# Hybrid RWKV-7, attention and gated-delta trunk on one core: merged recurrence tasks, given out in batches after a set wait, and a builder's clock that charges for changes of tile kind

## The chip, the core and the metric

One core of a Trainium2 chip. The metric is the device time of one execution in microseconds (us). The kernel before took 4177.51 us (median of 3 runs, 4175.42 to 4184.36).

## The reference, cut to what matters

Two layers. In each, one projection `x @ w_in` (1,024 to 4,240 columns) feeds three groups of heads. A layer norm follows the output projection. A prompt of 2,048 tokens and 8 running streams of 16 tokens (the "sample" part, 128 tokens) share the weights.

```
proj = x @ w_in
o_a = rwkv_mix(...)     # RWKV-7: state s <- s*w - (s.kk)(kk*a) + v k ; o = s.r, group norm, bonus
o_b = fox_prompt(...)   # softmax(q.k/8 + c_q - c_k), causal, 8 heads; sample: 1,024 cached rows each
o_c = gdn_mix(...)      # conv(4), silu, l2norm, delta rule in chunks of 64, RMS norm
h = concatenate([o_a, o_b, o_c]) @ w_out
x_new = layer_norm(ALPHA * x + h)
```

## The kernel before, in words

Each layer runs in three stages on TensorE. **Projection with recurrence:** `proj` walks over thirds of the tokens (640, 768, 768) and, for each block of 128 columns of `w_in`, makes 8 x 3 products of 128x128 by 384 (or 320) columns into the PSUM tile `pm`. The operands are split into a high and a low float32r part (`xh`, `xl`, `wh`, `wl`), hence three products. `vgroup` does the same by token block for the value columns (PSUM tile `pv`) and, during it, transposes the input of the next third (`pt`). **Attention:** `fox_prompt` makes `mx` (scores for the row maximum), `st` (scores again, shifted) and `fo` (weights by values). **Output:** `out_proj` makes `op` and the layer norm.

The recurrences of RWKV and gated delta (RG) and then the sample attention (`fox_sample`) are filled in between. They are written as generators, called tasks, one set per block of 256 tokens (`rg_sub`): `rwkv_a`, `gdn_a` prepare, `rwkv_b`, `rwkv_b2`, `gdn_b`, `gdn_b2` build small products, `inverse` and `inverse2` solve a triangular system, `both_chain` steps the state through 64-token chunks, and `rwkv_post`, `gdn_post` norm and gate the result. A task yields the time at which what it waits for is expected, and `step` gives out the next piece of the first task whose time has come.

What sets the order is the builder's own clock, `Model.t`. `PE.add` moves it on by a cost for each product; `Model.op` places every other engine's work against it and gives each instruction a priority from it. TensorE's instructions stay in the order in which the builder emits them during the first two stages; SyncE's DMA issues are ordered by the same clock. `drive` loops over the main work (projection or attention) and, when the clock passes `next_rg`, gives out one piece of a task, then lets the main work have as much of the clock as the piece took (`mix` is 1).

Tasks take PSUM from a ring `gr` of 2 banks for each of their tile names (all of one tag), and SBUF from rings by tag (`RG_TAGS`): `O` and `Ogc` shared one buffer, `Y` had another. Line 221 of the profile is `PE.matmul`, line 224 `PE.transpose`, line 243 every operation of the other engines; groups are therefore told by tiles.

The products of the tasks have several shapes. Of the TensorE rows, `64*64` means 64 rows of weights by 64 columns, `128*128` the whole array. Float32 products appear as two records each, transposes as one.

Of the kernel before, what the change touches and what calls it, by code (L numbers as in the profile page):

```python
# [78 lines left out]
for _tag, _bufs, _names in (  # L79
    ("t7", 1, "pr pc"),  # L80
    ("t7b", 1, "xs"),
    ("ur", 4, "sw a cs Dt kt"),
    ("uw", 1, "th sq n2"),
    ("ug", 2, "sg sqk gm Dm er"),
    ("ui", 1, "Wi T11"),
    ("uo", 1, "O Ogc"),
    ("uc", 1, "Oc so"),
    ("uz", 1, "z"),
    ("u9", 1, "Y"),
    ("m", 1, "strow lst lsto"),  # L90
    ("m2", 2, "lstc"),
    ("q4", 2, "BK DM N am rm km qm SSraw"),
):
    for _n in _names.split():
        RG_TAGS[_n] = (_tag, _bufs)
# [103 lines left out]
class PE:  # L199
    def __init__(self, tc, model):  # L200
        self.tc, self.eng, self.m = tc, tc.nc.tensor, model
        self.keep = False

    def add(self, fn, out, a, b, cyc, first):
        m = self.m
        m.t = max(m.t, m.ready(a, b))
        if first:
            m.t = max(m.t, m.last(out.tensor.name) + m.LAT if out.tensor.name not in m.done else 0.0)
        m.t += cyc / 2400.0
        for x in (a, b):  # L210
            m.used[x.tensor.name] = max(m.used.get(x.tensor.name, 0.0), m.t)
        m.done[out.tensor.name] = m.t + 0.05
        self.tc.cur_priority = int((m.t + 30.0) * 100)
        ins = fn()
        if self.keep:
            self.tc.keep_in_program_order(ins)
# [79 lines left out]
class Trunk:  # L296
# [236 lines left out]
    def proj(self, l, ti, groups, nxt=None):  # L533
# [35 lines left out]
        def vgroup(gi):  # L569
# [32 lines left out]
            if nxt is not None:  # L602
                for j in range(nt - 1, nn):
                    for k in range(2):
                        self.transpose_tile(l, nxt, j, k)
                        yield
# [168 lines left out]
    def rg_sub(self, l, t0, W):  # L775
# [24 lines left out]
        n["Er"] = self.task(self.rwkv_post(x), n["Dr"], n["Dg"], gate)  # L800
        n["Eg"] = self.task(self.gdn_post(x), n["Er"])
# [160 lines left out]
    def rwkv_b2(self, x):  # L962
# [5 lines left out]
        for p in range(2):  # L968
            ps = self.ps("gr", "bkp", 2)
            for c in range(nch):  # L970
                self.pe.transpose(ps[:, c * 128:c * 128 + 128], BK[:, p, c].rearrange("p s t -> p (s t)"), self.ident)
            nc.scalar.copy(BKt[:, p].rearrange("p c h t -> p (c h t)"), ps[:, :nch * 128])
        yield self.w(vv)
        X = self.rt("X", [128, 2, nch, 2, 64])
        ps = self.ps("gr", "vps", 2)
        for p in range(2):
            for w in range(nch // 2):
                q = p * (nch // 2) + w
                self.pe.transpose(ps[:, q * 128:q * 128 + 128], vv[:, p, w * 128:w * 128 + 128], self.ident)
        pv = ps[:, :nch * 128].rearrange("p (q w h t) -> p q w h t", q=2, h=2, t=64)  # L980
# [6 lines left out]
        yield self.w(X, Gk)  # L987
# [6 lines left out]
        Y = self.rt("Y", [128, 2, nch, 64])  # L994
        nc.scalar.copy(Y, yp)
        yield
        if not smp:
            lp = self.ps("gr", "l21", 2)[:, :npc * 32].rearrange("p (q c t) -> p q c t", q=2, t=32)
            for p in range(2):
                for c in range(nch):  # L1000
                    for h in range(2):
                        s = slice(h * 64, h * 64 + 64)
                        self.pe.matmul(lp[h * 64 + 32:h * 64 + 64, p, c], AR[s, p, c, 1, 32:64], BK[s, p, c, h, 0:32], start=True, stop=True)
            L21 = self.l21(x)
            for h in range(2):
                s = slice(h * 64 + 32, h * 64 + 64)
                nc.scalar.copy(L21[s, 0:npc], lp[s].rearrange("p q c t -> p (q c) t"))
        self.m.drop(BK)
        nc.gpsimd.tensor_tensor(kt, kt, r, op=ALU.mult)
        yield self.w(kt)  # L1010
        bp = self.ps("gr", "bonus", 2)[:, :2 * W].rearrange("p (q t) -> p q t", q=2)
        for p in range(2):
            self.pe.matmul(bp[:, p], v["rkm"][:, p], kt[:, p], start=True, stop=True)
        self.m.drop(kt)
# [5 lines left out]
    def gdn_a(self, x):  # L1020
# [61 lines left out]
        yield self.w(smt, sqk)  # L1082
        sp = self.ps("gr", "sps", 2)
        n4 = sp[:, 0:npc].rearrange("p (w q h) -> p w q h", q=2, h=2)
        for w in range(nch // 2):
            for p in range(2):
                self.pe.matmul(n4[:, w, p], sqk[:, p, w * 128:w * 128 + 128], self.k["bdones"][:, 0:128:64], start=True, stop=True)
        self.m.drop(sqk)
        kn, n2, be, ax, ab, g, b = (self.rt(nm, [128, nch, 2], 2) for nm in ("kn", "kn2", "be", "ax", "ab", "gg", "bb"))
        kv = kn.rearrange("p (w e) q -> p w e q", e=2)  # L1090
        for h in range(2):
            for e in range(2):
                nc.vector.tensor_scalar(kv[h * 64:h * 64 + 64, :, e], n4[e * 64:e * 64 + 64, :, :, h], L2_EPS, None, op0=ALU.add)
        nc.vector.tensor_tensor(ax, smt[:, :, 2:4], v["dt_bias"].unsqueeze(1).to_broadcast([128, nch, 2]), op=ALU.add)
        self.sigmoid(be, smt[:, :, 0:2])
        yield
        nc.vector.reciprocal(n2, kn)
        nc.scalar.activation(kn, kn, AF.Ln)
        nc.scalar.activation(kn, kn, AF.Exp, scale=0.5)
        nc.vector.tensor_tensor(b, be, n2, op=ALU.mult)  # L1100
# [5 lines left out]
        yield self.w(g)  # L1106
        gf = g.rearrange("p c q -> p (c q)")
        cp = self.ps("gr", "cps", 2)
        self.pe.matmul(cp[:, 0:npc], x["bdtri"], gf, start=True, stop=True)
        if not smp:  # L1110
            self.pe.matmul(cp[:, 64:64 + npc], self.k["bdtri32"], gf, start=True, stop=True)
        neg = self.rt("neg", [128, nch, 2], 2)
# [7 lines left out]
    def gdn_b(self, x):  # L1120
# [44 lines left out]
        L21 = None if smp else self.l21(x)  # L1165
        for c0 in range(0, nch, 2):
            ps = self.ps("gr", "eqp", 2)
            for c in (c0, c0 + 1):
# [6 lines left out]
            pk = ps.rearrange("p (j e t) -> p j e t", e=2, t=64)  # L1175
# [13 lines left out]
    def gdn_b2(self, x):  # L1189
# [9 lines left out]
        for src, dst in ((vv, Vt), (k, Kt)):  # L1199
            yield self.w(src)  # L1200
            ps = self.ps("gr", "vkp", 2)
            for p in range(2):
                for w in range(nch // 2):
                    j = w * 2 + p
                    self.pe.transpose(ps[:, j * 128:j * 128 + 128], src[:, p, w * 128:w * 128 + 128], self.ident)
            pv = ps[:, :nch * 128].rearrange("p (w q h t) -> p w q h t", q=2, h=2, t=64)
# [308 lines left out]
    def rwkv_post(self, x):  # L1515
        nc, v, W = self.nc, self.rv, x["W"]
        O, Oc = x["O"].rearrange("p q t -> p (q t)"), self.rt("Oc", [128, 2 * W])
        f = lambda t: t.rearrange("p (q t) -> p q t", q=2)
        yield self.w(O)
        mp = self.ps("gr", "mp", 2)[:, :2 * W]  # L1520
        self.pe.matmul(mp, self.k["bdones"], O, start=True, stop=True)
        nc.vector.scalar_tensor_tensor(out=Oc, in0=mp, scalar=-1.0 / 64.0, in1=O, op0=ALU.mult, op1=ALU.add)
        nc.scalar.activation(O, Oc, AF.Square)
        yield self.w(O)
# [3 lines left out]
        nc.scalar.activation(O, O, AF.Exp, scale=-0.5)  # L1528
        nc.vector.tensor_tensor(Oc, Oc, O, op=ALU.mult)
# [3 lines left out]
        self.gate(x, 0, f(Oc), "za")  # L1533
        nc.gpsimd.dma_start(self.OD[x["l"]][0:256, x["t0"]:x["t0"] + W].rearrange("(q p) t -> p q t", p=128), f(Oc))

    def gdn_post(self, x):
        nc, v, W = self.nc, self.rv, x["W"]
        O, Oc = x["Og"].rearrange("p q t -> p (q t)"), self.rt("Ogc", [128, 2 * W])
        f = lambda t: t.rearrange("p (q t) -> p q t", q=2)
        nc.scalar.activation(Oc, O, AF.Square)  # L1540
        nc.gpsimd.tensor_tensor(Oc, Oc, x["q2"].rearrange("p q t -> p (q t)"), op=ALU.add)
        yield self.w(Oc)
        mp = self.ps("gr", "gmp", 2)[:, :2 * W]
        self.pe.matmul(mp, self.k["bdones"], Oc, start=True, stop=True)
        nc.scalar.activation(Oc, mp, AF.Ln, bias=self.eps["gdn"], scale=1.0 / 64.0)
        nc.scalar.activation(Oc, Oc, AF.Exp, scale=-0.5)
        nc.vector.tensor_tensor(O, O, Oc, op=ALU.mult)
        nc.vector.tensor_scalar(O, O, v["gng"], None, op0=ALU.mult)
        self.gate(x, 768, f(O), "zc")
        nc.gpsimd.dma_start(self.OD[x["l"]][768:1024, x["t0"]:x["t0"] + W].rearrange("(q p) t -> p q t", p=128), f(O))  # L1550
# [519 lines left out]
```

## Time and profile before

| | |
|---|---|
| median of 3 runs | 4177.51 us |
| the profiled execution, its own time | 4169.68 us |
| its span in the profile | 4167.9 us |
| mean granted TensorE clock | 0.954 |
| TensorE busy | 3815.8 us (92%) |
| VectorE, ScalarE, GpSimd busy | 2710.4, 1637.5, 1243.3 us |

The profiled execution stands 7.8 us (0.19%) under the median. The stages of layer 0, by the first and last `pm`, `mx`, `st` and `op` in the trace: projection alone to about 200 us, projection with recurrence to 1351, attention with the rest of the tasks to 1922, output to 2121. Layer 1 follows with the same stages at 2250, 3404 and 3970 us. A busy TensorE row counts modelled ends, so what a product costs is read from start to start.

### The profile page before, as it was taken

How to read it: one execution, taken by the hardware profiler on the slowest of the kernel's cores; microseconds unless marked ns; L12 is line 12 of the kernel's file. 1: busy time of each engine (PE TensorE's matmuls, PEld its weight loads, DVE VectorE, ACT ScalarE, POOL GpSimd, SP SyncE). 2: the span in 40 equal slices, each digit the busy share in tenths (PEclk: the TensorE clock that was granted, in tenths of full speed). 3: DMA queues.
4: the chain of work that ended last, by engine and by line, in shares of the span. 5: the costliest groups of instructions: out<-in, count | busy, mean ns of one | idle time of the engine just before them, and what ended most of it. 6: DMA issues, size and time to landing. Idle time of an engine off the chain costs nothing.

```text
span 4167.9 us, 78031 instructions
## 1 busy us (share of the span) xinstructions
PE 3815.8 (92%) x30554; PEld 3058.0 (73%) x30554; DVE 2710.4 (65%) x6029; ACT 1637.5 (39%) x3351; POOL 1243.3 (30%) x1073
## 2 busy tenths in 40 slices
PE   5889998999988899989998898989999989999998
PEld 5878887888878455546888788978888864554477
DVE  5386567766775776774533857487578747777645
ACT  2253434344353344443123434244444514444411
POOL 3412232222121444444222112312121215444532
PEclk9899999999999899999999999989999989999999
DMA  7743545344544676463455445444445455764333
GB/s 241 222 150 118 151 147 172 117 136 145 161 152 149 155 210 181 119 154 100 150 156 174 150 122 158 154 141 141 135 142 162 155 156 173 197 190 123 88 114 121
DMA packets 601755, 633.81 MB, mean 152 GB/s; under 512 B 153625, under 2 KB 457483, under 8 KB 601387
## 3 DMA queue, kind: packets, MB, share of 16 engines
q1 hardware_dynamic: 598634, 619.90, 49.7%
q0 software_dynamic: 2752, 8.92, 0.6%
q8 instruction: 241, 3.95, 0.4%
q14 instruction: 128, 1.04, 0.1%
HBM read 437.59 MB, written 191.10 MB: 151 GB/s over the span
## 4 chain that ended last, share of the span: by engine, by line
PE 53%; DVE 21%; issue 11%; POOL 5%; DMA 5%; ACT 4%; SPq 1%; POOLq 0%; DVEq 0%; ACTq 0%
PE pm L221 22%; PE st L221 5%; PE fo L221 5%; PE op L221 4%; DVE Wi L243 3%; DVE itmp L243 3%; PE mx L221 3%; PE pv L221 2%; PE cr L221 2%; PE ktp L224 1%; DVE TT L243 1%; PE co L221 1%; PE cg L221 1%; DVE y L243 1%; DVE m L243 1%
## 5 line engine op out<-in xcount | busy, mean ns | idle before, releaser
L221 PE MATMUL pm<-xh,wh 128*128 128x384 f32 (+1 forms) x2784 | 1001.1, 360 | 34.0 <-ACT wh L243 29.1
L221 PE MATMUL pm<-xh,wl 128*128 128x384 f32 (+1 forms) x2784 | 928.7, 334 | 33.1 <-DMA wl<-wd 17.7
L221 PE MATMUL pm<-xl,wh 128*128 128x384 f32 (+1 forms) x2784 | 927.6, 333 | 0.0
L221 PEld LDWEIGHTS pm<-xh,wh 128*128 128x128 f32 x2784 | 537.5, 193 | 78.3 <-ACT wh L243 31.0
L221 PEld LDWEIGHTS pm<-xh,wl 128*128 128x128 f32 x2784 | 536.0, 193 | 38.7 <-DMA wl<-wd 20.2
L221 PEld LDWEIGHTS pm<-xl,wh 128*128 128x128 f32 x2784 | 538.0, 193 | 12.5 <-issue 12.1
L243 POOL TENSOR_TENSOR acc<-acc,pt 128x512 f32<-128x512 f32 (+2 forms) x336 | 382.0, 1152 | 339.9 <-ACT pt L243 307.1
L243 ACT ACTIVATE pt<-st 128x512 f32<-128x512 f32 (+3 forms) x640 | 331.2, 532 | 341.8 <-PE st L221 315.2
L243 DVE TENSOR_REDUCE m<-mx 128x1 f32<-128x512 f32 (+3 forms) x640 | 370.1, 603 | 131.1 <-PE mx L221 128.0
L243 ACT CAST wh<-wr 128x1024 fp32r<-128x1024 f32 (+1 forms) x198 | 207.9, 1051 | 287.4 <-PE pm L221 185.0
L221 PE MATMUL fo<-pt,V 128*64 128x512 f32 (+3 forms) x1280 | 313.3, 570 | 2.4 <-ACT pt L243 1.9
L243 ACT COPY st<-pm 128x384 f32<-128x384 f32 (+1 forms) x348 | 159.0, 458 | 385.6 <-PE pm L221 290.8
L221 PE MATMUL mx<-KA,QA 66*128 66x512 f32 (+3 forms) x640 | 265.1, 435 | 26.2 <-DMA QA<-qs 17.1
L221 PE MATMUL st<-QB,KB 128*128 128x512 f32 (+3 forms) x640 | 277.8, 434 | 8.0 <-DVE m L243 2.9
L221 PE MATMUL st<-QA,KA 104*128 104x512 f32 (+3 forms) x640 | 243.4, 380 | 1.1 <-DVE QA L243 1.1
L243 POOL TENSOR_SCALAR SD<-Sr,dl 128x64 f32<-128x64 f32 x128 | 68.3, 547 | 583.5 <-DVE Sr L243 547.7
L243 POOL TENSOR_TENSOR wl<-wr,wh 128x1024 fp32r<-128x1024 f32 x58 | 141.2, 2435 | 257.6 <-ACT wh L243 222.7
L221 PEld LDWEIGHTS mx<-KA,QA 66*128 66x128 f32 x640 | 126.9, 203 | 123.5 <-issue 78.8
L221 PE MATMUL op<-woh,oh 128*128 128x512 f32 x544 | 211.9, 389 | 0.0
L221 PE MATMUL op<-woh,ol 128*128 128x512 f32 x544 | 211.8, 389 | 0.0
L221 PE MATMUL op<-wol,oh 128*128 128x512 f32 x544 | 211.7, 389 | 0.0
L221 PEld LDWEIGHTS st<-QB,KB 128*128 128x128 f32 x640 | 128.6, 201 | 106.9 <-issue 65.4
(378 smaller groups left out, 7651.6 us busy)
## 6 DMA issues: line engine op xcount, KB each, us to landing
wr<-in_w_in SPq DMA_DIRECT2D x198, 512.0 KB
wl<-wd SPq DMA_DIRECT2D x116, 512.0 KB
kc<-in_cache_fox_k SPq DMA_DIRECT2D x32, 1024.0 KB
vc<-in_cache_fox_v SPq DMA_DIRECT2D x32, 1024.0 KB
wd<-wl SPq DMA_DIRECT2D x58, 512.0 KB
xin<-xd SPq DMA_DIRECT2D x78, 256.0 KB
y<-xd SPq DMA_DIRECT2D x34, 512.0 KB
ol<-od SPq DMA_DIRECT2D x34, 512.0 KB
```

Source lines behind the costliest of these rows:

```text
L221: self.add(lambda: self.eng.matmul(out, a, b, start=start, stop=stop), out, a, b, cyc, start)
L224: self.add(lambda: self.eng.transpose(out, a, ident), out, a, ident, 2 * numel(out), True)
L243: r = f(*a, **b)
```

## The change

Every engine has the same instructions as before (23,152 products on TensorE); their order and some waits differ.

- **Clock.** `PE.add` charges 280 cycles, in the builder's clock alone, where the kind changes: float32r or not, more than 64 rows or not, more than 64 columns or not.
- **Batches.** `drive` asks `due`: it starts a batch when the earliest ready task has been late for 1.5 us of that clock, or is late and no other task comes due within the next 1.5 us. It then gives out pieces until the batch has used 2 us.
- **Merged pieces.** `rwkv_post` and `gdn_post` are one task `post` (it waits for `gdn_b2` too). In `rwkv_b2` the products `l21` move ahead of `yps`, and `bonus` follows `yps` at once. In `gdn_a` the products for the norms and for the cumulated decay come together. `gdn_b` makes both halves of `eqp` before it reads either; `gdn_b2` makes both transposes together. `vgroup` makes the two halves of the next third's transposes in one place (k = 4) instead of two (k = 1 and 5).
- **Buffers.** `Ogc` moves from `O`'s buffer to `Y`'s.

TensorE, the projection during the second block of the prompt. `cr` and `cg` are products of the state chain (`both_chain`), `eqp` of `gdn_b`, `pm` is the main work. Before, a step of the chain is a visit by itself, and each half of `eqp` (`x8`) another, six `pm` ahead of these rows' end and six behind it:

```order
L221 MATMUL pm<-xh,wh 128x384
L221 MATMUL pm<-xl,wh 128x384
L221 MATMUL pm<-xh,wl 128x384
L221 MATMUL cr<-X,BKt 64x64 x4
L221 MATMUL cg<-Xg,Kt 64x64 x4
```

Now:

```order
L224 MATMUL pm<-xh,wh 128x384
L224 MATMUL pm<-xl,wh 128x384
L224 MATMUL pm<-xh,wl 128x384
L224 MATMUL cr<-R,TT 64x64 x4
L224 MATMUL cg<-Rg,TT 64x64 x4
L224 MATMUL eqp<-y 64x128 x16
```

Three visits became one: a step of the chain and both halves of `eqp`.

TensorE, the projection of the value columns, first block of the prompt; `sps` and `cps` are products of `gdn_a`, `yps` and `bonus` of `rwkv_b2`, `pt` the transposes of the next third. Before, `cps` is a visit by itself, and so are `sps` and `yps` ahead of it and `bonus` behind it:

```order
L224 MATMUL pt<-cst,xin 128x128 x4
L221 MATMUL pv<-wh,xh 128x256
L221 MATMUL pv<-wl,xh 128x256
L221 MATMUL pv<-wh,xl 128x256
L221 MATMUL cps<-gg,cst 128x8 x2
```

Now:

```order
L227 MATMUL pt<-cst,xin 128x128 x8
L224 MATMUL pv<-wh,xh 128x256
L224 MATMUL pv<-wl,xh 128x256
L224 MATMUL pv<-wh,xl 128x256
L224 MATMUL sps<-cst,sqk 128x2 x4
L224 MATMUL sps<-gg,cst 128x8 x2
L224 MATMUL yps<-X,Gk 64x64 x16
L224 MATMUL bonus<-kt,rkm 128x256 x2
```

Four visits became one, and `pt` stands eight at a time.

TensorE, the last block of a layer: `mp` and `gmp` are products of the post task, `sfp` of the state's output, `mx` the attention's first maxima. Before:

```order
L221 LDWEIGHTS idb
L221 MATMUL mx<-ngb,idb 128x128
L224 MATMUL sfp<-cst,Sr 64x128 x2
L221 MATMUL mx<-KA,QA_14837 128x512
L221 MATMUL mp<-O,cst 128x512
L221 MATMUL mx<-KA,QA_14837 128x128
```

Now:

```order
L224 MATMUL pm<-xh,wh 128x320
L224 MATMUL pm<-xl,wh 128x320
L224 MATMUL pm<-xh,wl 128x320
L224 MATMUL mp<-O,cst 128x512
L224 MATMUL gmp<-Ogc,cst 128x512
```

The recurrence of a layer now ends inside the projection.

The diff, cut to its core:

```diff
     def add(self, fn, out, a, b, cyc, first):
         m = self.m
+        kind = (a.dtype == F32R, a.shape[0] > 64, out.shape[0] > 64)
+        if kind != self.kind:
+            cyc, self.kind = cyc + 280.0, kind
         m.t = max(m.t, m.ready(a, b))
...
     def drive(self, fill):
         for until in fill:
             if until:
                 self.idle(until)
-            while self.m.t >= self.next_rg:
-                t = self.m.t
-                if not self.step():
-                    break
+            t = self.m.t
+            if t >= self.next_rg and self.due(t):
+                while self.m.t - t < 2.0 and self.step():
+                    pass
                 self.next_rg = self.m.t + self.mix * (self.m.t - t)
+
+    def due(self, t):
+        wakes = [self.wake(q) for q in self.tasks if q.ready()]
+        late = t - min(wakes, default=t + 1.0)
+        return late >= 0.0 and (late >= 1.5 or not any(t < w <= t + 1.5 for w in wakes))
...
-                    if nxt is not None and k in (1, 5):
-                        if j:
-                            self.transpose_tile(l, nxt, j - 1, k // 5)
-                        if j < nn:
-                            self.xin[l, nxt, j, k // 5] = self.load_x(l, nxt, j, k // 5)
+                    if nxt is not None and k == 4:
+                        for half in range(2):
+                            if j:
+                                self.transpose_tile(l, nxt, j - 1, half)
+                            if j < nn:
+                                self.xin[l, nxt, j, half] = self.load_x(l, nxt, j, half)
...
-        n["Er"] = self.task(self.rwkv_post(x), n["Dr"], n["Dg"], gate)
-        n["Eg"] = self.task(self.gdn_post(x), n["Er"])
+        n["Er"] = n["Eg"] = self.task(self.post(x), n["Dr"], n["Dg"], n["Bg2"], gate)
...
-        yield self.w(X, Gk)
+        if not smp:
+            L21 = self.l21(x)
+            for h in range(2):
+                s = slice(h * 64 + 32, h * 64 + 64)
+                nc.scalar.copy(L21[s, 0:npc], lp[s].rearrange("p q c t -> p (q c) t"))
+        self.m.drop(BK)
+        yield self.w(X, Gk, kt)
...
-        yield self.w(smt, sqk)
-        sp = self.ps("gr", "sps", 2)
...
+        yield self.w(g, sqk)
+        cp = self.ps("gr", "sps", 2)
...
+        eqs = []
         for c0 in range(0, nch, 2):
             ps = self.ps("gr", "eqp", 2)
+            eqs.append(ps)
...
+        yield self.w(O, Ogc)
+        mp, gp = self.ps("gr", "mp", 2)[:, :2 * W], self.ps("gr", "gmp", 2)[:, :2 * W]
         self.pe.matmul(mp, self.k["bdones"], O, start=True, stop=True)
+        self.pe.matmul(gp, self.k["bdones"], Ogc, start=True, stop=True)
```

## Rows read from the trace of the kernel before

**Rows 1.** The page's first part: the span, and TensorE's busy time.

```profile
span 4167.9 us, 78031 instructions
PE 3815.8 (92%) x30554; PEld 3058.0 (73%) x30554; DVE 2710.4 (65%) x6029; ACT 1637.5 (39%) x3351; POOL 1243.3 (30%) x1073
```

**Rows 2.** Busy time by stretch: us, PE, PEld, DVE, ACT, POOL, granted clock, DMA share, GB/s.

```profile
200.00:1351.00 1151.00, 1059.83 (x10390) 961.57 (x10391) 782.23 (x2047) 489.94 (x1050) 243.52 (x249) 0.95 0.48 146
1351.00:1457.00 106.00, 87.36 (x427) 46.54 (x426) 77.12 (x145) 35.29 (x66) 50.83 (x48) 0.82 0.60 154
1457.00:1770.00 313.00, 302.84 (x2173) 167.60 (x2173) 228.11 (x432) 150.27 (x286) 135.71 (x118) 0.99 0.61 171
1770.00:1922.00 152.00, 137.13 (x586) 68.67 (x584) 105.75 (x162) 72.99 (x134) 87.16 (x72) 0.93 0.43 110
```

**Rows 3.** TensorE's timeline, a visit to 64*64 tiles: start us, us to the end, what.

```profile
439.33 0.40 PE L221 MATMUL co<-qe,Sg 64*64 64x64 f32 x8
439.56 0.40 PE L221 MATMUL co<-Eq,Xg 64*64 64x64 f32 x8
439.89 0.45 PE L221 MATMUL pm<-xh,wh 128*128 128x384 f32 x1
440.18 0.34 PE L221 MATMUL pm<-xl,wh 128*128 128x384 f32 x1
440.36 0.34 PE L221 MATMUL pm<-xh,wl 128*128 128x384 f32 x1
...
442.83 0.34 PE L221 MATMUL pm<-xl,wh 128*128 128x384 f32 x1
443.01 0.34 PE L221 MATMUL pm<-xh,wl 128*128 128x384 f32 x1
443.28 0.45 PE L221 MATMUL cr<-Sr,AR 64*64 64x64 f32 x8
443.56 0.40 PE L221 MATMUL cg<-Sg,y 64*64 64x64 f32 x8
```

**Rows 4.** TensorE's timeline, visits of 4 and 8 transposes on the whole array.

```profile
384.79 0.60 PE L224 MATMUL vkp<-cst,yv 128*128 128x128 f32 x4
...
385.41 0.34 PE L221 MATMUL pm<-xl,wh 128*128 128x384 f32 x1
...
391.14 1.04 PE L224 MATMUL bkp<-cst,BK 128*128 128x128 f32 x8
...
392.19 0.34 PE L221 MATMUL pm<-xl,wh 128*128 128x384 f32 x1
```

**Rows 5.** TensorE's waits from 200 to 1351 us: total us, times, longest.

```profile
PE pt L224 <- DMA xin<-xd: 9.0, 2, 4.8
...
PE vkp L224 <- ACT X L243: 5.6, 1, 5.6
PE gps L221 <- DVE Gr L243: 5.3, 1, 5.3
...
PE cg L221 <- DVE Sg L243: 0.2, 1, 0.2
```

**Rows 6.** TensorE's timeline, one such wait (in brackets: idle us before it, and what ended it).

```profile
915.00 1.11 PE L224 MATMUL vkp<-cst,y 128*128 128x128 f32 x4 [5.62 <-ACT X L243]
```

**Rows 7.** Busy time by stretch around that wait, columns as in rows 2.

```profile
905.00:912.70 7.70, 4.37 (x27) 4.00 (x25) 7.10 (x22) 1.08 (x3) 1.25 (x1) 1.00 0.44 138
912.70:919.60 6.90, 4.60 (x16) 4.45 (x16) 6.37 (x18) 6.42 (x15) 2.00 (x3) 0.51 0.32 104
919.60:930.00 10.40, 10.40 (x113) 9.78 (x112) 9.64 (x24) 3.81 (x7) 2.24 (x2) 1.00 0.31 97
```

**Rows 8.** Timeline, a hand-off in the sample attention: scores, exponential, transposes.

```profile
1672.92 0.23 PE L221 MATMUL sqn<-kx,qbd 128*32 128x16 f32 x8
...
1676.10 1.15 ACT L243 ACTIVATE S<-S,sfm 128x1040 f32<-128x1040 f32 x1
...
1679.99 0.77 PE L224 MATMUL ptp<-cst,S 128*128 128x128 f32 x5
```

More of the change, by code (lines that the diff above doesn't have):

```diff
@@ L986, in rwkv_b2 @@
                 nc.scalar.copy(Xw[d, :, :, e, h], pv[s, :, :, h])
-        yield self.w(X, Gk)
+        if not smp:
+            L21 = self.l21(x)
+            for h in range(2):
+                s = slice(h * 64 + 32, h * 64 + 64)
+                nc.scalar.copy(L21[s, 0:npc], lp[s].rearrange("p q c t -> p (q c) t"))
+        self.m.drop(BK)
+        yield self.w(X, Gk, kt)
         yp = self.ps("gr", "yps", 2)[:, :npc * 64].rearrange("p (q c t) -> p q c t", q=2, t=64)
@@ L1105, in gdn_a @@
         nc.vector.tensor_tensor(g, g, v["a_log"].unsqueeze(1).to_broadcast([128, nch, 2]), op=ALU.mult)
-        yield self.w(g)
+        yield self.w(g, sqk)
+        cp = self.ps("gr", "sps", 2)
+        n4 = cp[:, 128:128 + npc].rearrange("p (w q h) -> p w q h", q=2, h=2)
+        for w in range(nch // 2):
+            for p in range(2):
+                self.pe.matmul(n4[:, w, p], sqk[:, p, w * 128:w * 128 + 128], self.k["bdones"][:, 0:128:64], start=True, stop=True)
+        self.m.drop(sqk)
         gf = g.rearrange("p c q -> p (c q)")
-        cp = self.ps("gr", "cps", 2)
         self.pe.matmul(cp[:, 0:npc], x["bdtri"], gf, start=True, stop=True)
@@ L1111, in gdn_a @@
             self.pe.matmul(cp[:, 64:64 + npc], self.k["bdtri32"], gf, start=True, stop=True)
+        kv = kn.rearrange("p (w e) q -> p w e q", e=2)
+        for h in range(2):
+            for e in range(2):
+                nc.vector.tensor_scalar(kv[h * 64:h * 64 + 64, :, e], n4[e * 64:e * 64 + 64, :, :, h], L2_EPS, None, op0=ALU.add)
+        nc.vector.reciprocal(n2, kn)
+        nc.scalar.activation(kn, kn, AF.Ln)
+        nc.scalar.activation(kn, kn, AF.Exp, scale=0.5)
+        nc.vector.tensor_tensor(b, be, n2, op=ALU.mult)
         neg = self.rt("neg", [128, nch, 2], 2)
@@ L1174, in gdn_b @@
                         self.pe.matmul(ps[s, jj * 128:jj * 128 + 128], k[s, p, cs], y4[s, p, 0:2, cs], start=True, stop=True)
-            pk = ps.rearrange("p (j e t) -> p j e t", e=2, t=64)
+        for c0 in range(0, nch, 2):
+            pk = eqs[c0 // 2].rearrange("p (j e t) -> p j e t", e=2, t=64)
             j = slice(c0 * 2, c0 * 2 + 4)
@@ L1198, in gdn_b2 @@
         Vt, Kt = self.rt("Vt", [128, npc, 64]), self.rt("Kt", [128, npc, 64])
-        for src, dst in ((vv, Vt), (k, Kt)):
-            yield self.w(src)
+        yield self.w(vv, k)
+        two = []
+        for src in (vv, k):
             ps = self.ps("gr", "vkp", 2)
+            two.append(ps)
             for p in range(2):
@@ L1205, in gdn_b2 @@
                     self.pe.transpose(ps[:, j * 128:j * 128 + 128], src[:, p, w * 128:w * 128 + 128], self.ident)
+        for ps, dst in zip(two, (Vt, Kt)):
             pv = ps[:, :nch * 128].rearrange("p (w q h t) -> p w q h t", q=2, h=2, t=64)
@@ L1532, in rwkv_post @@
         nc.gpsimd.tensor_tensor(f(Oc), f(Oc), x["bv"], op=ALU.add)
[L1533 to L1550, printed above, removed]
+        for r0, y in ((0, f(Oc)), (768, f(Og))):
+            self.gate(x, r0, y, "z")
+            nc.gpsimd.dma_start(self.OD[x["l"]][r0:r0 + 256, x["t0"]:x["t0"] + W].rearrange("(q p) t -> p q t", p=128), y)
     def fx_fill(self, eng, KA, QA):
```

60 lines of the change are left out of this document (21 added, 39 removed).

## The prediction

> **What bounds the kernel now.** I read the page's engine shares first, then the stretches, then TensorE's timeline and its waits. TensorE is busy 92% of the span [rows 1]; no other engine comes near. By stretch [rows 2] that holds where the change acts: 1059.83 of 1151 us in the projection with recurrence, 302.84 of 313 us where the sample attention fills the prompt's attention. Where nothing fills it, it is less: 137.13 of 152 us at the end of the attention, and 87.36 of 106 us at its start. So time can be won in three ways: less lost on TensorE between products, fewer waits of TensorE, and a granted clock that stays up (0.95 in the projection, so a tenth of that stretch ran at the lower of the two levels, 1.2 GHz).
>
> No instruction is added or removed on any engine, DMAs included. What moves is the order, and the sum below is made against the profiled execution (4169.7 us), for one layer and then doubled.
>
> **Changes of tile shape.** A visit to 64*64 tiles and back can be read to the end [rows 3]. Products of `pm` follow each other by 0.18 us (442.83 to 443.01), but the first task product starts 0.27 us behind the last `pm`, 0.09 too much. Its group of four takes 0.28 to the next group, where 0.23 is usual (439.33 to 439.56): 0.05 more. On the way back the last group takes 0.33 instead of 0.23, and the first `pm` 0.29 instead of 0.18: 0.21 more. A visit there and back costs 0.35 us, a change 0.175.
>
> A visit whose products use the whole array costs nothing of the kind [rows 4]. Four transposes and the `pm` behind them take 0.62 us (384.79 to 385.41), eight and a `pm` 1.05 (391.14 to 392.19). So four transposes take 0.43; and 0.43 + 0.18 is 0.61, which leaves 0.01 for going and coming. The Trainium skill, in "TensorEngine Tiling (Array Packing)", section Key Properties, says that TensorE drains when the tiling mode changes, not when only the tile does. The trace agrees on both sides, 0.35 us against 0.01. By that rule the builder's new charge is wrong in half of its cases, those that change the type alone. The builder would count 446 kinds fewer in the program (3,223 to 2,777), at its 280 cycles of 2.4 GHz an estimated 52 us, where the sum below has 26.
>
> Counted in the two built orders, a layer's projection stage has 315 visits before and 203 after, but 470 changes of tile shape before and 408 after: most visits that go were on the whole array (merged transposes, `post`, `sps` with `cps`) or stood beside another. 62 x 0.175 is 10.9 us a layer. In the attention the changes fall from 398 to 389 in layer 0 and 383 in layer 1, 12 on average: 2 us.
>
> **Waits at the start of a visit.** TensorE waits 91 us in 200 to 1351 us of layer 0. 61 of them are in 23 rows of task tiles, from `vkp` with 5.6 to `cg` with 0.2 us; 30 in 8 rows of main work, from `pt` (9.0) down [rows 5]. A third fewer visits (112 of 315) would take 22 us of the 61 if each visit were as likely to wait as before; 0 if the waits hang on the work and not on how often one asks. Batches wait for up to 1.5 us of the builder's clock, which gives the first piece more room; the pieces behind it get none, and the clock now runs faster against TensorE's work, which takes room away. I take 10 us of gain, near the middle, since neither row decides.
>
> **The clock behind a wait.** The 5.62 us wait of `vkp` [rows 6] is followed by 6.9 us at 0.51 of the clock, with 1.00 before and 1.00 after [rows 7]: 2.4 GHz, then 1.2, then 2.4, and what the engine did before it fell was wait. At 0.95 over 1151 us, some 115 us are at the lower level; at most half, 58 us, is lost. Two thirds of the waits are the tasks', so 38 us. Where waits fall by 10 of 61, I take the same sixth: 6 us. Bounds: 0 and 14 (the third of the 38).
>
> **What the attention loses.** Tasks now end earlier. Before, the recurrence's last products stood among the first 67 of the 1,536 products of the attention, and the sample ran from product 134 to 1,074. After, the recurrence ends 27 products ahead of the attention's start, and the sample runs from 50 to 854. Products without anything beside them go from 67 + 462 to 50 + 682, 203 more. What that costs is read from the two stretches [rows 2]: unfilled, TensorE is idle 15 of 152 us (9.8%) at a clock of 0.93; filled, 10 of 313 (3.2%) at 0.99. Idle is 6.6% more, and a clock lower by 0.06 costs up to 6%. 152 us hold 462 products, 0.33 us each; 203 are 67 us, and 12.6% of it 8 us. Bounds: 0, if the last rows wait for VectorE anyway, and 15.
>
> The filled part gets tighter too. In one hand-off of the sample [rows 8], the scores start at 1672.92, the exponential ends at 1677.25 (1676.10 + 1.15), and the transposes come at 1679.99: 2.7 us to spare out of 7. The new order leaves fewer products between such pairs: 16 rows between `sqn` and `ptp` instead of 26 in the third sequence of layer 0. Room of 2.7 us covers most of it. I take 4 us a layer; bounds 0 and 15.
>
> **Edits at nothing.** The merged `eqp`, `vkp` and `mp` with `gmp` take both banks of ring `gr` at once, so the next task's product waits until one is read; TensorE has main work behind it in the queue, which that wait holds up, and this is inside the wait term. The transposes of the input take two of four banks in one place; each is read as before, and its loads are issued as far ahead. `Ogc` in `Y`'s buffer is written after the chain that reads `Y`. SyncE's queue and GpSimd's have the same issues, placed by the same clock; with TensorE the bound and GpSimd busy 244 of 1151 us [rows 2], I take nothing for them. If the weights were issued late, `pm` would wait, as it does now for some microseconds in rows like those of main work in rows 5.
>
> **The sum.** A layer: -10.9 - 2 - 10 - 6 + 8 + 4 = -16.9 us; two layers -34. 4169.7 - 34 = 4136; the profiled execution stands 7.8 us under the median shown, so 4144 us against 4177.5, 0.8% faster. With the bounds, a layer goes from -10.9 - 2 - 22 - 14 = -49 to -12.9 + 15 + 15 = +17: 4080 to 4212 us.
>
> **Rivals.** *The waits go with the visits* (chance 0.16): 112 fewer visits take their third of waits and of the low clock, and the attention loses little. -10.9 - 2 - 22 - 14 + 8 is -41 a layer, 4096 us. For it: 61 us of small waits with 23 causes. Against it: merged pieces ask for more at once.
>
> *The clock charges too much and the hand-offs come too early* (0.15), the slower side. The builder counts 280 cycles for each change between float32r and float32 or bfloat16 on the whole array, which rows 4 show to be free (there are over 500 such changes with the mask product alone). It then believes more time has gone by than has, and puts a consumer closer behind its producer. The room of 2.7 us [rows 8] would go first. The sample has some 14 hand-offs in each of 8 sequences; if a third of these 112 wait 0.5 us and six of the waits bring the clock down as in rows 7 (some 3.4 us lost each), that is 19 + 20 us; with the lost fill 8 and the gain of 12.9, +34 a layer: 4246 us at worst, 4207 at half the hand-offs. It decides from the point at which room falls under the queueing on VectorE, which is busy 73% there (228 of 313 us) [rows 2].
>
> *Nothing to measure* (0.16): the kinds it saves are free ones, the shape changes save 26 us, and lost fill with tighter hand-offs takes it back: 4170 to 4180 us. For it: rows 4, and that most visits saved are on the whole array.
>
> **The numbers.** The forecast has the rest, 0.53. About 0.2% is what a measurement of this kernel can tell from no change, 8 us. Faster by more: nearly all of the forecast (0.50), the first rival (0.16) and a little of the third (0.03): 0.69. Slower by more: the second rival and a little of the third, 0.15. Within: 0.16. The range from 4090 to 4205 holds the forecast's costs to near both bounds, the first rival at its sum and the third, and leaves out most of the second.
>
> **What would show it.** Right: the projection stretches shorten from 1151 to about 1125 us; `pm` behind `eqp` or `cr` in fewer places; TensorE's waits there near 80 instead of 91 us; the last stretch without the sample longer than 152 us by some 70 (220 products at 0.33 us), at a clock of 0.93 or less. Wrong: waits of `ptp`, `sfo`, `sft`, `rrp` that grow to over 20 us a layer (the second rival); waits in the projection as large as before under other names, which would leave only the 26 us; or `pm` waiting for weights, which I gave nothing.

## The result, and the profile after

The changed kernel takes 4298.01 us (median of 4 runs, 4286.16 to 4306.39) against 4176.47 us before (4 runs beside it, 4167.91 to 4184.36): 1.0287 times as long, with an interval of 1.0266 to 1.0308, 121.5 us more. The forecast was 4144 us, in a range up to 4205: wrong in its sign, and by 154 us. The profiled execution took 4306.39 us, 136.7 more than the one before; it was the slowest of its four runs, and the profiled one before a fast one, so what the two profiles show below is some 15 us more than the medians.

The first part of the page of the changed kernel answers to [rows 1]. TensorE is busy 31 us longer in a span that is 137 us longer: most of the loss shows as idle time, and time at the lower clock counts as busy.

```profile
span 4304.6 us, 78238 instructions
PE 3846.6 (89%) x30554; PEld 3096.4 (72%) x30554; DVE 2720.0 (63%) x6029; ACT 1635.0 (38%) x3351; POOL 1230.4 (29%) x1073
```

By stretch, with the columns and the meaning of [rows 2] (projection; attention's start; attention with the sample; attention without it), after:

```profile
200.00:1381.00 1181.00, 1064.95 (x10512) 974.34 (x10512) 795.07 (x2063) 492.18 (x1059) 246.47 (x251) 0.95 0.47 143
1381.00:1457.00 76.00, 49.86 (x205) 27.64 (x204) 47.10 (x96) 19.88 (x37) 30.47 (x35) 0.69 0.76 190
1457.00:1750.00 293.00, 268.24 (x1995) 150.21 (x1993) 200.29 (x379) 133.61 (x253) 112.72 (x99) 0.98 0.63 176
1750.00:1987.00 237.00, 212.46 (x861) 104.70 (x862) 155.56 (x246) 101.27 (x186) 120.89 (x101) 0.87 0.32 84
```

In layer 0 the projection went from 1151 to 1181 us, the attention from 571 to 606; the output stage stayed. Layer 1 repeats it (1283 to 1312 and 567 to 605). So a layer lost some 30 us in its projection and 35 to 38 in its attention. The attention of layer 0 as one stretch, before and after:

```profile
1351.00:1922.00 571.00, 527.32 (x3183) 282.80 (x3181) 410.98 (x738) 258.55 (x485) 273.69 (x237) 0.94 0.56 151
1381.00:1987.00 606.00, 530.56 (x3059) 282.56 (x3058) 402.96 (x719) 254.76 (x475) 264.07 (x234) 0.90 0.52 142
```

**Projection.** TensorE's waits there (total us, times, longest) sum to 121 us in 39 rows, where [rows 5] had 91 in 31. The sum counts a little twice: TensorE's idle time went from 91 us (1151 less 1059.83) to 116 (1181 less 1064.95), and in layer 1 from 108 to 126. The largest after:

```profile
PE pv L224 <- DMA wl<-wd_v: 17.4, 2, 10.4
PE gps L224 <- DVE BK L246: 9.3, 3, 5.3
PE bkp L227 <- DVE L L246: 8.8, 7, 1.8
PE nps L224 <- ACT sq L246: 7.9, 2, 5.1
PE cr L224 <- DVE X L246: 7.7, 2, 4.7
PE cr L224 <- DVE R L246: 7.1, 3, 3.5
```

The main products now wait for the low part of the value weights (`wl<-wd_v`, 1.1 us before), and the tasks' products for the vector and scalar engines at more places: 83 us of the 121 are theirs, where it was 61 of 91. The granted clock is 0.95, as before. And 122 rows more stand in this stretch (10512 against 10390): the end of the recurrence, which was in the attention.

**Attention.** Waits rose from 42 to 75 us. Two rows make all of the difference, before:

```profile
PE rrp L224 <- DVE rr L243: 14.6, 11, 3.1
PE mx L221 <- DMA QA<-qs: 8.7, 3, 5.6
```

after:

```profile
PE rrp L227 <- DVE rr L246: 32.8, 22, 4.1
PE mx L224 <- DMA QA<-qs: 23.5, 5, 8.4
```

`rrp` is the transpose that hands the row maxima of the prompt's attention on (`fx_shift`). `ptp` and `sfo`, the sample's hand-offs that I named, do not wait at all. The second row is the load of the prompt's queries; 15.8 of its 23.5 us fall in the first 76 us of the attention, where the recurrence's end used to stand. The longest `rrp` wait on TensorE's timeline after (start, duration, what; idle time and its end in brackets):

```profile
1905.35 0.50 PE L224 MATMUL mx<-KA,QA 66*128 66x512 f32 x1
1905.69 0.34 PE L224 MATMUL st<-QB,KB 128*128 128x384 f32 x1
1905.87 0.34 PE L224 MATMUL st<-QA,KA 104*128 104x384 f32 x1
1906.04 0.23 PE L224 MATMUL st<-idb,ngb 128*128 128x128 bf16 x1
1910.37 0.37 PE L227 MATMUL rrp<-cst,rr 128*8 128x128 f32 x1 [4.09 <-DVE rr L246]
```

and on the vector engine's:

```profile
1905.89 0.69 DVE L246 TENSOR_REDUCE m<-mx 128x1 f32<-128x512 f32 x1 [0.74 <-PE mx L224]
1906.50 0.15 DVE L246 TENSOR_REDUCE m<-m 128x4 f32<-128x12 f32 x1
1907.01 1.23 DVE L246 TENSOR_TENSOR ol<-ol,oh 128x1024 fp32r<-128x1024 f32 x1 [0.36 <-ACT oh L246]
1908.15 0.96 DVE L246 TENSOR_SCALAR rr<-m 128x4 fp32r<-128x4 f32 x1
1909.03 1.21 DVE L246 TENSOR_TENSOR ol<-ol,oh 128x1024 fp32r<-128x1024 f32 x1
1910.16 0.15 DVE L246 SCALAR_TENSOR_TENSOR rr<-m,rr 128x4 fp32r<-128x4 f32 x1
```

The builder put `rrp` as the fourth product behind the last maximum. The vector engine needs four steps for `rr`, has two additions of 1.2 us for the output weights (`ol`) among them, and is done 4 us later; TensorE's queue stands. The windows around that wait show what follows it (columns as in [rows 2]):

```profile
1906.30:1910.40 4.10, 0.03 (x2) 0.03 (x2) 3.66 (x6) 2.11 (x3) 1.92 (x2) 0.84 0.15 38
1910.40:1917.40 7.00, 7.00 (x24) 4.12 (x25) 3.81 (x7) 1.05 (x3) 0.46 (x1) 0.50 0.08 22
1917.40:1925.00 7.60, 7.60 (x24) 3.50 (x23) 3.11 (x5) 2.07 (x4) 0.58 (x2) 0.50 0.16 49
```

For at least 14.6 us TensorE then runs busy at 1.2 GHz, half its speed. The attention's mean clock fell from 0.94 over 571 us to 0.90 over 606: 69 us at the lower level became 121, and half of the difference, at most 26 us, is lost. Waits +33, clock +26, less 124 rows that moved out (at the stretch's mean of 0.17 us, an estimated 21 us) gives 38, against 35 measured.

### The profile page after: what moved, and what is told of

The parts are those of the page before. It is cut to its first block, busy times and chain, and to the rows that moved or that the text cites. A ratio compares the mean times of both kernels' runs of the same rounds, so it can differ in the third digit from the quotient of the medians.

```text
span 4304.6 us, 78238 instructions
## 1 busy us (share of the span) xinstructions
PE 3846.6 (89%) x30554; PEld 3096.4 (72%) x30554; DVE 2720.0 (63%) x6029; ACT 1635.0 (38%) x3351; POOL 1230.4 (29%) x1073
## 4 chain that ended last, share of the span: by engine, by line
PE 50%; DVE 19%; issue 12%; DMA 8%; POOL 5%; ACT 4%; SPq 1%; POOLq 0%; DVEq 0%; ACTq 0%
PE pm L224 20%; PE st L224 5%; PE op L224 5%; PE fo L224 4%; PE pv L224 3%; PE mx L224 3%; DVE Wi L246 2%; DVE itmp L246 2%; DVE y L246 2%; SPq L246 1%; PE cr L224 1%; PE co L224 1%; PE ktp L227 1%; DVE m L246 1%; PE cg L224 1%
## 5 line engine op out<-in xcount | busy, mean ns | idle before, releaser
L224 PE MATMUL pm<-xh,wh 128*128 128x384 f32 (+1 forms) x2784 | 982.5, 353 | 31.3 <-ACT wh L246 26.3
L224 PE MATMUL mx<-KA,QA 66*128 66x512 f32 (+3 forms) x640 | 276.2, 458 | 66.0 <-DMA QA<-qs 48.0
L224 PE MATMUL fo<-pt,V 128*64 128x512 f32 (+3 forms) x1280 | 322.0, 584 | 1.2 <-DVE fu L246 1.2
```

Of the source, the lines that this page charges most:

```text
L224: self.add(lambda: self.eng.matmul(out, a, b, start=start, stop=stop), out, a, b, cyc, start)
```

## The experiments

Theories 1, 2 and 3 are the parts of the change: the charge, the batches with the set wait, the merged pieces. All times are medians; the ratio is to runs of the kernel before on the same chip.

| run | edit | us | ratio (interval) |
|---|---|---|---|
| e1 | charge alone | 4244.9 | 1.0164 (1.0144 to 1.0185) |
| e2 | batches and set wait alone | 4222.6 | 1.0115 (1.0098 to 1.0133) |
| e3 | merged pieces alone | 4160.7 | 0.9965 (0.9945 to 0.9985) |
| e4 | the change without the charge | 4220.1 | 1.0112 (1.0091 to 1.0132) |
| e5 | charge, projection only | 4203.4 | 1.0069 (1.0047 to 1.0091) |
| e6 | charge, attention only | 4247.7 | 1.0181 (1.0158 to 1.0205) |
| e7 | batches without the set wait | 4216.1 | 1.0102 (1.0079 to 1.0126) |
| e8 | the change, `mix` 1.5 in the projection | 4287.8 | 1.0272 (1.0250 to 1.0295) |
| e9 | e2, `mix` 1.3 in the projection | 4186.0 | 1.0034 (1.0016 to 1.0051) |
| e10 | before, attention priced at 0.8 | 4182.2 | 1.0023 (1.0006 to 1.0040) |
| e11 | e6, attention priced at 0.8 | 4214.5 | 1.0097 (1.0068 to 1.0126) |
| e12 | e3, attention priced at 0.8 | 4141.9 | 0.9920 (0.9891 to 0.9949) |
| e13 | e6, shape changes only | 4221.0 | 1.0107 (1.0077 to 1.0137) |
| e14 | e6, type changes only | 4245.9 | 1.0161 (1.0135 to 1.0186) |
| e15 | the change, no charge in the attention, `mix` 1.3 | 4229.9 | 1.0135 (1.0094 to 1.0176) |
| e16 | e12, `mix` 1.15 in the projection | 4173.2 | 0.9981 (0.9967 to 0.9995) |
| e17 | the change, `rrp` due 2.5 us later | 4256.0 | 1.0188 (1.0162 to 1.0215) |
| e18 | e12, `rrp` due 2.5 us later | 4140.4 | 0.9921 (0.9895 to 0.9947) |

**e1 to e4: the parts.** e1 adds the three lines on `kind` to the kernel before, e2 the new `drive` and `due`, e3 the merged pieces and buffers, e4 is the change without those three lines.

> The kernel before, with the builder's charge for changes of kind alone (tasks and giving out as before). Theory 1, the charge makes the loss: the builder's clock runs ahead of TensorE, consumers stand closer behind their producers and the sample ends at product 854 of the attention instead of 1,074. Then this kernel is slower than before by most of the 121 us: 4250 to 4290 us. Theory 2, the batches make it: 4165 to 4190 us. Theory 3, the merged pieces make it: 4165 to 4190 us.

> The kernel before, with batches and the set wait alone. 401 changes of tile shape in a layer's projection instead of 470. Theory 1: no loss, or a gain of the shape changes, 4150 to 4185 us. Theory 2, batches make long stretches in which TensorE has only task products and waits inside them, and the recurrence's end moves out of the attention: 4240 to 4290 us. Theory 3: 4150 to 4185 us.

> The kernel before, with the merged pieces, the transposes in one place and the moved buffer alone. 447 changes of tile shape instead of 470. Theory 1 and theory 2: 4155 to 4185 us. Theory 3, merged pieces take both banks of the ring at once and make the next product wait: 4230 to 4290 us.

> The changed kernel without the charge (batches and merged pieces stay). 405 changes of tile shape, the sample ends at product 983 of the attention. Theory 1: close to or under the kernel before, 4140 to 4190 us. Theory 2 and theory 3: most of the loss stays, 4250 to 4300 us.

The charge alone costs 69 us and the batches alone 47; the merged pieces save 15. So no theory holds by itself: e1, e2 and e4 lie between the ranges of "makes the loss" and "makes none", and only e3 settles its own, theory 3, against it. e4, +44, shows that the batches undo what the merged pieces gain. The three parts make +101 one by one, the change +121 together.

**e5, e6: where the charge costs.** The charge is switched off outside one stage (the line against e1's; the switch is set where the attention begins and ends):

```diff
-            cyc, self.kind = cyc + 280.0, kind
+            cyc, self.kind = cyc + (280.0 if self.charge else 0.0), kind
```

> The kernel before with the charge for changes of kind, as in e1, but only until the attention begins; the attention is built at the old prices. By the written order the recurrence ends 30 products before the attention (as in e1), the sample's products reach product 973 of the attention's 1,536 (e1 854, before 1,074). Theory F (what costs is that the recurrence is used up before the attention, so that its first 70 us have no other work beside them): the attention's head is lost as in e1, its tail only in part; attention 590 to 597 us a layer against 572, whole kernel 4205 to 4230. Theory P (what costs is that the raised clock of TensorE puts the hand-offs inside the attention too early): nothing is charged there, 4165 to 4185.

> The kernel before with the charge only from the attention's begin to its end. The projection is that of before; the recurrence still has 64 products of the attention beside it, the sample's work ends at product 940 instead of 1,074. Theory F: only the tail loses cover, 134 products of 0.33 us at some 13 per cent, 6 us a layer, up to 12: 4185 to 4200. Theory P: the whole loss of e1 is here, 4230 to 4250.

Each stage's charge has a cost, +30 and +74; they do not add up, since e1 has both and costs 69. Cover is work of the tasks that stands beside the attention's own. e6 speaks against lost cover as the main reason: its recurrence still ends in the attention, and it costs as much as e1, as theory P has it. Its attention has 603 us (before 571) with the sample's work ending 134 products earlier. Its stretch, and its waits for the row maxima, which are those of the change:

```profile
1351.00:1954.00 603.00, 535.25 (x3186) 287.10 (x3185) 416.02 (x739) 258.87 (x486) 270.19 (x238) 0.93 0.53 143
```

```profile
PE rrp L227 <- DVE rr L246: 31.0, 21, 4.6
```

e5, 4203 us, lies just under the range of theory F. Its projection is 8 us longer, by 120 rows that moved into it (10510 against 10390). Its attention has as many rows less, an estimated 20 us of work at 0.17 us each, and nothing charged, yet it is not shorter (575 us); it waits 59 us instead of 42:

```profile
1359.00:1934.00 575.00, 518.59 (x3064) 277.24 (x3064) 400.21 (x722) 251.27 (x470) 261.05 (x232) 0.93 0.55 149
```

```profile
PE rrp L227 <- DVE rr L246: 20.7, 17, 3.5
PE mx L224 <- DMA QA<-qs: 15.9, 4, 11.3
```

So the early end of the recurrence has a cost too, and it is paid in the attention.

**e7 to e9: batches, and where the recurrence ends.** e7 drops `self.due(t)` from e2's condition; e8 (in the change) and e9 (in e2) alter one number, to 1.5 and 1.3:

```diff
-            self.pe.keep, self.mix, self.ring = True, 1.0, ((f"psR{l}", "gr"), 2)
+            self.pe.keep, self.mix, self.ring = True, 1.3, ((f"psR{l}", "gr"), 2)
```

> The kernel before with the batches of 2 us in the builder's clock, but no set wait: a batch begins as soon as a task is ready, as before. The written order has 225 visits in the projection (e2 211, before 315), and the recurrence ends before the attention as in e2. If the batches cost (several pieces one behind the other, so that the waits for DVE and ACT come close behind each other, and the recurrence runs ahead of the projection): 4210 to 4230, as e2. If it is the set wait that costs: 4165 to 4190.

> The whole change, with one number altered: during the projection the main work gets 1.5 times a batch's time before the next batch, instead of 1.0. The written order has 180 visits in the projection (203), and the recurrence ends 102 products into the attention, its samples at product 940 (before: 67 and 1,074; change: 27 products ahead of the attention, 854). Theory F: the attention is back at 575 to 590 us a layer from 606, and the waits of the projection stay: whole kernel 4225 to 4260. If the loss of the change hangs on the charged clock or the batches themselves, wherever the recurrence ends: 4285 to 4310.

> Batches and set wait as in e2, but with 1.3 times a batch's time for the main work during the projection, instead of 1.0. The written order then ends the recurrence 100 products into the attention (before 67, e2 27 projection products ahead of it) and the samples at product 1,082 (before 1,074, e2 983). Theory F for the batches (their loss is the place to which they bring the recurrence's end, as in e5, which cost 30 us by that alone): 4175 to 4195. Theory B (the loss is in the batches themselves: pieces close behind each other wait for DVE and ACT): 4210 to 4230.

e7 is as slow as e2: what costs is the batch, not the set wait. e9 recovers 33 of e2's 47 us when the recurrence ends in the attention again, though not in the stage expected: its projection is 16 us shorter than before (1135, with 43 rows less), its attention 21 longer (592, with 48 more). Together with e5 this parts e2's loss: the early end without batches costs 30 us (e5), batches without the early end 14 (e9), both 47 (e2). e5's charge in the projection and e9's wider spacing stand in these numbers too, so the parting is rough. The wait for the queries at the attention's start goes with it: 5.6 us before and 6.0 in e9; 13.8 in e2, 15.1 in e5, 15.8 in the change and 15.7 in e17. In e2 the value weights are late as in the change; in e9 that row is gone:

```profile
PE pv L221 <- DMA wl<-wd_v: 14.5, 4, 8.9
```

e8 is a miss of the same theory: with the recurrence's end back in the attention the whole change still costs 114 us, 121 without the edit, and the attention's charge is there as before (633 us of attention, with 162 rows more than before).

**e10 to e12: the price of the attention.** In `PE.add`, with `rate` 0.8 during the attention and 1.0 elsewhere:

```diff
-        m.t += cyc / 2400.0
+        m.t += cyc * self.rate / 2400.0
```

> The kernel before, with TensorE's instructions priced at 0.8 of their old price in the builder's clock during the attention, and nothing charged for kinds. That moves the samples' pieces the opposite way to e6: their work ends at product 1,268 of 1,536 (before 1,074, e6 940), with more products between two steps of one task. Theory S (e6 lost 37 us a layer because a clock that runs faster per product uses the samples' work up earlier, brings its hand-offs closer in products, and leaves a longer bare tail): the attention gets shorter by 8 to 25 us a layer, 4125 to 4160. If e6 lost because of where single charges fall, or if the attention of before stands at its optimum: 4165 to 4200.

> e6 (charge for kinds in the attention alone) with all of TensorE's prices there, the charge among them, taken times 0.8, so that the attention has about its old length in the builder's clock. By the written order the samples end at product 1,090 (before 1,074, e6 940). The charge is still there, relative to the other prices. Theory S (the total of the clock counts): 4165 to 4190. Theory L (the charge itself, on 850 instructions an attention of which 500 change only the number type, puts single pieces in worse places): 4225 to 4250.

> e3 (the merged pieces alone) with the attention priced at 0.8 as in e10; samples end at product 1,268. Theory S: e3's gain of 15 us and e10's add up, 4110 to 4145. Otherwise 4155 to 4185.

e10 missed: more cover at the end and more products between hand-offs win nothing over the kernel before (attention 575 us, waits for `rrp` 18 where they were 14.6). e11 lies between the two theories: 32 of e6's 74 us come back, and its `rrp` waits fall to 18.5 us. e12, 4141.9 us, is 0.8% under the kernel before, and only e18, a variant of it, is as fast. It falls in theory S's range, though not by its sum, since e10 had no gain to add:

```profile
200.00:1335.00 1135.00, 1046.85 (x10344) 950.40 (x10342) 783.01 (x2037) 488.03 (x1051) 240.62 (x248) 0.96 0.49 148
1335.00:1907.00 572.00, 523.43 (x3232) 282.69 (x3232) 411.33 (x749) 259.99 (x486) 271.08 (x239) 0.95 0.55 151
```

It keeps e3's shorter projection and brings the attention from e3's 589 us to 572.

**e13, e14: which charges.** `kind` is cut to its two shape terms, or to its type term, in e6.

> e6 (charge in the attention alone) with only real changes of the tile's shape charged, some 350 an attention, 41 us of the builder's clock; the 500 instructions that change only the number type are free, as the trace has them. Samples end at product 985 (before 1,074, e6 940). If the charges on the number type did the harm: 4170 to 4195. If each charged 0.117 us costs alike, the loss of 74 splits as 41 to 58 and this run loses some 31: 4195 to 4215. If the shape charges did it: 4225 to 4250.

> The complement of e13: in the attention only changes of number type are charged, whether or not the shape changes with them. Samples end at product 955. If the charges on the number type did the harm: 4225 to 4250. If each charge costs alike: 4210 to 4235. If the shape charges did it: 4170 to 4195.

e13 lies between its ranges, e14 in the one for harm by the types. Either half of the charge does more than half of the harm (39 and 64 of 74), so the two do not add up. The waits for `rrp` rise with the clock that is charged: 14.6 us before, then e13 and e14:

```profile
PE rrp L227 <- DVE rr L246: 24.3, 16, 4.9
```

```profile
PE rrp L227 <- DVE rr L246: 32.3, 20, 4.3
```

and the attention goes with them: 571, 594, 605 us. In other runs it does not: e10 and e12, priced at 0.8, wait 18 us for `rrp` at 575 and 572 us, and e16 waits 12 at 591 (with 160 rows more than e12). By [rows 4] the type charges are the false ones (0.01 us for going and coming). The Trainium skill, in "TensorEngine Tiling (Array Packing)", section Key Properties, has TensorE drain when the tiling mode changes; [rows 4], where it does not change, agree. e13 shows that the charges on shapes cost time too, so falseness alone is not the reason.

**e15, e16: are the parts the whole, and is cover the gain.**

> The whole change (merged pieces, batches with the set wait, the charge in the projection), with the two suspected causes taken away: no charge inside the attention, and 1.3 times a batch's time for the main work in the projection, which puts the recurrence's end at product 88 of the attention and the samples' at 1,082 (before 67 and 1,074). If the parts found are the whole loss and add up: batches as in e9 +14, merged pieces as in e3 -15, 4160 to 4190. If something is left that only the three together make: 4205 to 4260.

> e12 with 1.15 times a step's time for the main work in the projection: the recurrence ends 137 products into the attention (e12 88) and the samples at product 1,339 (e12 1,268, e3 1,074). If cover that lasts longer is what made e12 faster than e3: 4110 to 4140. If e12's gain was the chance of one order, or cover at 1,268 is enough: 4140 to 4175.

e15 recovers 73 of the 121 us and leaves 48, outside the range for "the parts add up" and inside the one for something that only the three together make. Its projection still waits 108 us in 1153, and its two attentions, of the same instructions, last 622 and 591 us:

```profile
1353.00:1975.00 622.00, 567.23 (x3311) 302.62 (x3310) 418.73 (x753) 260.14 (x488) 275.40 (x242) 0.88 0.51 139
3470.00:4061.00 591.00, 541.35 (x3311) 290.02 (x3310) 419.50 (x752) 259.43 (x487) 275.29 (x240) 0.93 0.54 146
```

31 us between twins: 0.88 against 0.93 of the clock is 26 of them, the busy time's difference. This profiled execution was the slowest of the four by 26 us, so the pair shows how much the clock alone can move, not what e15 costs. e16 puts the samples' end at product 1,339 and is, by the two ratios, 0.6% slower than e12: cover that lasts longer is not what made e12 fast.

**e17, e18: the one hand-off.** In `fx_shift`:

```diff
-        return self.w(rr), run, (h, b)
+        return self.w(rr) + 2.5, run, (h, b)
```

> The whole change, and the transposes rrp (the hand-off of the row maxima in the attention) due 2.5 us later in the builder's clock than the vector engine's result; the samples' end stays (product 843, change 854), so cover is the same. Theory H (the charge harms the attention because its own hand-offs come too early in products): rrp's waits fall from 33 to under 15 us an attention, the granted clock rises, and the whole gets 30 to 70 us shorter, 4230 to 4270. If the waits only go along with the lost cover: they turn up at the next product, 4280 to 4310.

> e12 with the same 2.5 us on rrp. The samples end at product 1,267 (e12 1,268). Theory H: rrp's 18 us of waits an attention fall below 8, and the whole gets 10 to 30 us shorter than e12, 4110 to 4132. If the waits turn up elsewhere: 4135 to 4160.

e17, the whole change with this one line, loses its waits for `rrp` and gets its clock back:

```profile
PE mx L224 <- DMA QA<-qs: 17.9, 5, 8.4
PE mx L224 <- DVE m L246: 9.5, 8, 3.4
PE rrp L227 <- DVE rr L246: 4.1, 2, 3.5
```

```profile
1385.00:1955.00 570.00, 514.04 (x3064) 271.50 (x3064) 403.01 (x723) 254.44 (x476) 267.77 (x236) 0.95 0.55 151
```

The attention is back from 606 to 570 us (from 605 to 577 in layer 1), with the sample's work still ending 11 products earlier than in the change. The whole is 42 us shorter by the medians; the two attentions say 64, but the change's profiled execution was its slowest and e17's its fastest. So this one hand-off, with the clock behind it, makes some 42 us of the loss, with cover as it was. It does not clear the lost cover: e17's attention has 119 rows less than the one before, an estimated 20 us of work, and still takes as long; it waits 55 us instead of 42, and the queries at its start are as late as in the change. What is left of the loss is 82 us by the medians; in the profile the projections are longer by 34 and 31 us, with some 120 moved rows in each, and the attentions by -1 and 9. In e12, whose waits for `rrp` were 18 us, the same line takes them to 3.0 and wins nothing:

```profile
PE rrp L224 <- DVE rr L243: 3.0, 3, 1.2
```

All waits of the attention fall by 6 us alone (48 to 42), since `st` and others wait a little later instead, and the attention stays at 574 us, at 0.94 of the clock (e12 0.95).

## Why the prediction was wrong

**Two steps failed.** The costlier one is the term for the tighter hand-offs, "I take 4 us a layer; bounds 0 and 15". The charge in the attention alone costs 74 us, 37 a layer (e6), and one hand-off, `rrp`, carries some 42 us of the whole change's loss (e17).

The other is **the term for the waits**, "I take 10 us of gain, near the middle, since neither row decides". Its bounds were 0 and 22 us of gain; a loss was not among them, although the same paragraph said that the pieces behind a batch's first "get none" of the room. Measured: TensorE is idle 25 us more in the projection of layer 0 and 18 more in that of layer 1. No part does this alone (idle there in layer 0: e3 85, before 91, e1 91, e2 101, e4 101, the change 116). e7 shows that of e2's 47 us the batch itself, not the set wait, brings the cost; most of that goes when the recurrence ends in the attention again (e9), but not the idle time in the projection (99 us).

Term by term, a layer:

- **Shape changes, -10.9 and -2.** No run isolates it. In the projection of layer 0, +25 of idle time, 122 rows more at that stretch's 0.10 us (an estimated +12) and -10.9 would make +26, against 30 measured: the term fits, which is not proof.
- **Waits, -10.** +25 and +18, as above.
- **The clock behind waits, -6.** 0 in the projection (0.95 both times, which two digits tell to some 6 us); the cost fell in the attention, up to 26 us. The price of one such wait was read too high: in [rows 7] the low stretch begins 2.3 us before the wait ends (912.7 against 915.0), and TensorE is busy for 4.6 of its 6.9 us, so 2.3 us were lost there and not 3.4.
- **Lost fill, +8, bounds 0 and 15.** The bare end of the attention came nearly as forecast: 237 us for 152 (forecast 70 more), at 0.87 of the clock. But e17 has the same early end, an attention of 570 us and a clock of 0.95, so most of the low clock came with `rrp` and not with the want of cover (e5, with the early end and nothing charged in the attention, has 0.93). The early end itself is worth some 30 us, 15 a layer, by e5, e9 and e2: the term's upper bound, and in waits, of which e5's attention has 16 us more in layer 0, 7 of them for the queries at its start. The term counted the start as 17 bare products fewer (67 to 50) and had no price for queries that come late there.
- **Tighter hand-offs, +4, bounds 0 and 15.** The right mechanism at the wrong place and far too small. I looked at the sample's pair in [rows 8], with 2.7 us to spare; the prompt's own `rrp` had none: before the change it already waited 14.6 us in 11 places. With the clock behind its waits it costs 21 us a layer by the medians (e17 against the change; 36 and 28 in the profiled executions).

**The rivals.** The second, with 0.15, had sign and cause: charges that bring consumers too close, each long wait followed by a low clock. It gave 34 us a layer at worst; the attention alone lost 35. It named the type charges as the false ones, and they hurt more (e14 +64, e13 +39), but the true ones hurt as well. It did not have the batches, and the projection's 30 us were in no rival. The first rival (waits go with the visits) fell with the 121 us of waits; the third with the result. Of the signs of error that I listed, all came in some form: `rrp` over 20 us a layer; waits in the projection not smaller, but larger, under other names; and main work that waits for weights (`pv`, 17.4 us), to which I had given nothing.

**What stays open.** In the projection of layer 0 the change waits 121 us, e4 108, e2 101, e1 96, e3 91. Which single piece of the order turns 108 into 121 when the charge is added was not tried. Nor has a cause been found for the 48 us that e15 leaves, without the early end and without the attention's charge. It is also open why e12's attention is 17 us shorter than e3's, since neither longer cover (e16) nor looser `rrp` (e18) adds to it. Kernels that differ by one number, as e12 and e16, differ by 0.6%, some 13 us a layer, so gains of that size from one order are not evidence for a rule.

## What to carry to other kernels

When a builder's clock sets the order, a correction of its prices moves every consumer against its producer: here +74 us from a charge in one stage. First look for the hand-off that already waits. Giving it room by its own due time gave 42 us back where low clock followed its waits (e17), and nothing where the clock was at 0.95 anyway (e18). Merge small pieces (-15 us), but do not take for granted that giving out several in a row helps: batches alone cost 47 us, most of it, as e5 and e9 part it, because they used up the work that had covered the next stage. And price a wait with the low clock that follows it, not by its own length.

## What the hardware showed that I had not expected

- A wait of 4.1 us on TensorE was followed by 14.6 us at 1.2 GHz with TensorE busy throughout: up to 7.3 us lost behind 4.1 us of waiting.
- The same instructions in the same order took 622 us in one layer and 591 in the other (e15), by the granted clock (0.88 and 0.93), in the slowest of four executions.
